# Streaming encoder layer on one core: the last two groups of h made beside the first four attention tiles, and the projections of the first unit given out on another plan

## The chip, the core and the metric

The kernel runs on one core of a Trainium2 chip. The metric is the device time of one execution in microseconds; the time of a kernel is the median over its runs. A separate execution is recorded by the hardware profiler, and all views below are of that one.

The engines are named as in the profile: PE is TensorE (matmuls; PEld its weight loads), DVE is VectorE, ACT is ScalarE, POOL is GpSimd, SP is SyncE, which here issues nearly all transfers, one after the other, on its own queue (SPq).

## The reference

One layer of a streaming encoder. 2048 new frames of one prompt, and 16 further frames of each of 8 running streams with 512 cached frames, go through the same weights.

```python
h, gate = adaln_modulate(x, c, norm_g, w_ada, b_ada)   # rms norm, then scale and shift per sequence
qa, ka, va, za, qb, kb, vb, zb, ga, gb = split(h @ w_in)
qa, ka = rope(qa, pos), rope(ka, pos)
oa = diff_attention(qa, ka, va, lam)            # 4 heads: softmax minus lambda times a second softmax
ob = stick_breaking_attention(qb, kb, vb)       # 8 heads: sigmoids and a running product of 1 - sigmoid
oa = rms_norm(oa, subln_g) * (1 - lam_init)
ya = (oa * silu(za)) @ w_branch_a
yb = (ob * silu(zb)) @ w_branch_b
x = x + gate * ((sigmoid(ga) * ya + sigmoid(gb) * yb) @ w_out)
y = rms_norm(x, final_g)
```

The outputs are y and the new keys and values of both branches. All tensors are 32-bit floats. The kernel keeps that precision on 16-bit matmuls: each operand is split into a high and a low half, and a product is the sum of three matmuls.

## The kernel before

**Tiles and units.** The prompt is 16 tiles of 128 rows; the 128 rows of the running streams are a seventeenth (index 16, `NT`). The heads are done in 8 units (`units`), in turn one diff-attention head and a pair of stick-breaking heads. A *step* is one tile of one unit; the list `steps` takes in each unit the sample tile first and then tiles 0 to 15, so step 0 is the sample tile of unit 0, step m (1 to 16) is tile m - 1 of unit 0, and step 17 begins unit 1: 136 steps.

**Projection.** `project` makes a step in 12 *pieces* of two matmuls of 512 columns (L423), 24 in all, into one of two PSUM banks ("mm"). In odd units 12 more pieces of two matmuls make a block of gate columns (L495). When the 24 are done, `finish` turns the bank into outputs and 16-bit operands: ScalarE copies (L437) and splits (L287, L450), VectorE makes the low halves (L292, L451), GpSimd does the rotation (L457 to L462), and three stores go out on SyncE's queue. `transpose_qk` (L508 to L519) turns q and k during the next step; its results for q live in six buffers (`Q_BUFS`).

**Where h comes from.** h, transposed and split, is made in the first stage in groups of four tiles. `normed(g)` sums squares and scales the rows of x (L1049). `modulated(g)` has eight pieces, one for each 128 columns: four transposes on TensorE (L1070), two ScalarE operations (L1076, L1077), one of VectorE (L1078). They fill one of two 16 KB buffers (`hp`); after the eighth piece SyncE writes the group to DRAM (`hT_d`, L1087). The projections of the first stage read h straight from `hp`, by the table `at_hand`; all others read it back into one of three buffers (`hs`) by `fetch_h` (L400). While `at_hand` is empty, each step issues the reading of the next one at its third piece (`H_AT`). Groups 0 and 2 share one `hp` buffer, 1 and 3 the other, so group 3 can be written only when the projections of tiles 4 to 7 have read theirs.

**Attention.** `attention(n)` returns two lists: the scores of step n (`scores`, L630 to L634; VectorE takes them out of PSUM, L545; softmax and weights on ScalarE and VectorE, L120, L594, L287, L292), and the products with V (`pv`, L678 to L683) of step n - 2 (`PV_LAG`). Between them the weights are transposed by a transfer on SyncE's queue (L568). In the first stage the scores of a tile lie in two of the four free weight buffers (`early_sc`), even tiles in one pair, odd ones in the other; later in a pool of its own.

**The order.** All pieces of projection stand in one list, `line`. `position(x)` is the place in it where step x begins, with a fraction for a part of a step. `take(target, need)` gives out pieces up to a target, or further if a tile's attention would otherwise lack its operands. `interleave` merges several lists in proportion to given costs. That fixes the order of the program. The framework's scheduler then orders each engine's instructions by a simulated timeline, with the program's order as priority, so that an instruction that is ready can go ahead of earlier ones that are not.

**The first stage** (`P0_AT`, `P0_STEPS`) makes groups 0 and 1 of h beside the projections up to position 5. Then, for each of attention tiles 0 to 7, it interleaves: a quarter of `modulated(2)` (two pieces) for tiles 0 to 3, a quarter of `modulated(3)` for tiles 4 to 7; `normed(3)` beside the first four; the last two parts of the modulation from `w_ada` (`gates`) beside tiles 4 and 6; and the pieces of projection up to the next target of `P0_STEPS`. At its end three tiles are read back by `fetch_h`.

**After it**, the loop over n from 9 gives each attention step its projections up to a target that follows a planned time: `past` adds a duration for each step so far, `pace` is that share of all 136 steps, and the target is `LEAD` (5) steps further. `prepare_unit(1)`, which loads unit 1's weights, sums their squares and cuts them in halves (L319, L321, L274, L289, L292), is given out over n = 9 to 12. The first four weight buffers it loads into are those that held the scores of the first stage.

Of the kernel before, what the change touches and what calls it, by code (L numbers as in the profile page):

```python
# [32 lines left out]
NT = SEQ // P  # L33
# [10 lines left out]
W_FIRST = 12  # L44
WIDE_BUFS = 6
P0_AT = 1.0, 5.0
P0_STEPS = 6.0, 7.0, 8.0, 9.0, 10.0, 11.0, 11.5, 12.0
K_BUFS = 6
V_BUFS = 23
S_TILES = 13  # L50
# [4 lines left out]
LEAD = 5.0  # L55
# [55 lines left out]
def layer_kernel(ctx: ExitStack, tc: tile.TileContext, a: dict):  # L111
# [751 lines left out]
    def position(x):  # L863

        m = min(int(x), len(steps) - 1)
        return starts[m] + (starts[m + 1] - starts[m]) * (x - m)

    def take(target, need):

        i = at[0]  # L870
        out = []
        while i < len(line) and (i < target or any(m <= need for m, _ in line[i : i + 14])):
            out.append((1.0, line[i][1]))
            i += 1
        at[0] = i
        return out
# [17 lines left out]
    with tc.tile_pool(name="p0", bufs=1) as p0:  # L894
# [136 lines left out]
        def normed(g):  # L1031

            t0, w = GROUPS[g]
            nt = w // P

            def square(i):
                if i == 0:
                    ss[g] = p0.tile([P, 4], F32, tag="ss", name="ss", bufs=2)
                sum_squares(xs[g][i], D, ss[g][:, i : i + 1])
                if i == nt - 1:  # L1040
                    ss[g] = rsqrt(ss[g], nt, D, p0, "rstd")

            def scale(i):
                x = xs[g][i]
                r = ss[g][:, i : i + 1]
                if g == 0 and i % 2:
                    V.tensor_scalar(out=x, in0=x, scalar1=r, scalar2=None, op0=ALU.mult)
                else:
                    G.tensor_scalar(out=x, in0=x, scalar1=r, scalar2=0.0, op0=ALU.mult, op1=ALU.add)  # L1049

            if g not in xs:
                xs[g] = load_x(t0 // P, nt)
            squared = [] if g in ss else [(0.5, lambda i=i: square(i)) for i in range(nt)]
            return squared + [(1.0, lambda i=i: scale(i)) for i in range(nt)]
# [36 lines left out]
        def gates():  # L1091

            def last():
                gateT = p0.tile([P, KT, 9], F32, name="gateT")
                V.tensor_tensor(out=gateT, in0=mod[:, 16:24, :],
                                in1=wide(bgT[:, 16:24]), op=ALU.add)
                gr = wide_tile().rearrange("p k n -> p (k n)")
                for n in range(2):
                    pt = bank("s")
                    for j in range(4):  # L1100
                        T.transpose(pt[0:9, j * P : (j + 1) * P], gateT[:, n * 4 + j, :], ident)
                    V.tensor_copy(out=gr[0:9, n * 512 : (n + 1) * 512], in_=pt[0:9, :])
                load(out=gate_d, in_=gr[0:9, 0:D])

            def piece(n):
                modulation(n)
                if n == 5:
                    last()

            return [(1.0, lambda n=n: piece(n)) for n in (4, 5)]  # L1110
# [7 lines left out]
        del free[:]  # L1118
        attention(0)
        for t, to in enumerate(P0_STEPS):  # L1120
            if t % 4 == 0:
                work, beside = modulated(2 + t // 4), normed(3) if t == 0 else gates()
            i = t % 4
            m = len(beside) // 4
            some = beside[i * m : i * m + m] if m else beside[i // 2 : i // 2 + 1] if i % 2 == 0 else []
            interleave(work[2 * i : 2 * i + 2], some, take(position(to), t + 2), *attention(t + 1))

        at_hand.clear()
        for m in range(3):
            fetch_h(*steps[int(P0_STEPS[-1]) + m])  # L1130

    free += early_sc
    del early_sc[:]
# [5 lines left out]
    whole = sum(duration(t) for _, t in steps)  # L1139
    first_step = len(P0_STEPS) + 1  # L1140
    past = sum(duration(t) for _, t in steps[:first_step])
    back += prepare_unit(1)
    cuts = None
    branch_weights = list(range(8))
# [125 lines left out]
    for n in range(first_step, len(steps) + PV_LAG):  # L1270
        if n < len(steps):
            u, t = steps[n]
            past += duration(t)
            if t == NT and u < 7:
                back += prepare_unit(u + 1)
            if u == 7 and not back and not spare and len(branch_weights) > 1:
                branch_weight()
            if back:
                for fn in back[: -(-len(back) // max(1, (W_READY if u else W_FIRST) - t % NT))]:
                    back.pop(0)()  # L1280
            else:
                for _ in spare[: -(-len(spare) // ((NT + 1 - t % NT) + 8 * (6 - min(u, 6))))]:
                    spare.pop(0)()
        qk, vs = attention(n)
        target = position(len(steps) * past / whole + LEAD)
        pieces = take(target, min(n + 1, len(steps) - 1))
        if at[0] == len(line) and not pieces and not spare:
            if cuts is None:
                cuts = early_work()
            pieces = [(1.0, fn) for fn in cuts[: -(-len(cuts) // (len(steps) + PV_LAG - n))]]  # L1290
            del cuts[: len(pieces)]
        interleave(pieces, qk, vs)
# [123 lines left out]
```

## Time and profile before

| | |
|---|---|
| median of 3 runs | 2296.72 us (2291.05 to 2299.35) |
| the profiled execution | 2301.96 us, span 2300.1 us |
| mean granted TensorE clock | 0.962 |
| busy: PE, DVE, ACT, POOL | 91%, 70%, 64%, 30% |
| last piece of h, group 3, written out from | 174.25 us |
| first projection with unit 1's weights | 223.60 us |
| first scores of unit 1 | 307.86 us |

A view by stretches gives the busy time of each engine between two times, counted from the first instruction; PEclk is the TensorE clock that was granted, 1.00 being full. In a timeline a line is a start, a duration, the engine, the source line, the operation, output and inputs, and in brackets the idle time of the engine just before with what ended it. A matmul's duration reaches into the next one's, so matmuls are compared by their spacing. In a list of waits the columns are the total, the number of times and the longest.

### The profile page before, as it was taken

How to read it: one execution, taken by the hardware profiler on the slowest of the kernel's cores; microseconds unless marked ns; L12 is line 12 of the kernel's file. 1: busy time of each engine (PE TensorE's matmuls, PEld its weight loads, DVE VectorE, ACT ScalarE, POOL GpSimd, SP SyncE). 2: the span in 40 equal slices, each digit the busy share in tenths (PEclk: the TensorE clock that was granted, in tenths of full speed). 3: DMA queues.
4: the chain of work that ended last, by engine and by line, in shares of the span. 5: the costliest groups of instructions: out<-in, count | busy, mean ns of one | idle time of the engine just before them, and what ended most of it. 6: DMA issues, size and time to landing. Idle time of an engine off the chain costs nothing. (4 is left out here: it accounts for less than half of the span.)

```text
span 2300.1 us, 40624 instructions
## 1 busy us (share of the span) xinstructions
PE 2088.9 (91%) x14478; PEld 1111.0 (48%) x14478; DVE 1609.4 (70%) x3523; ACT 1482.1 (64%) x2968; POOL 688.5 (30%) x575
## 2 busy tenths in 40 slices
PE   4997998998999899899989989999986789888997
PEld 2554554554555455455545555555553344444443
DVE  4576866689786677978666798877778655555554
ACT  3876767678776677777667787766776444444431
POOL 1522012345300234530023464113344222232331
PEclk7998999999999999999999999999997899999998
DMA  8659658597775768875566887657687979887662
GB/s 293 209 139 259 169 126 223 143 203 180 195 158 125 164 143 194 183 192 134 116 163 145 198 182 174 150 137 162 149 185 174 300 216 260 209 218 199 185 154 74
DMA packets 764555, 412.98 MB, mean 180 GB/s; under 512 B 525530, under 2 KB 709130, under 8 KB 763840
## 3 DMA queue, kind: packets, MB, share of 16 engines
q1 hardware_dynamic: 763274, 409.91, 72.7%
q8 instruction: 113, 1.85, 0.3%
q14 instruction: 90, 0.74, 0.1%
q10 hardware_dynamic: 1078, 0.48, 0.1%
HBM read 212.58 MB, written 72.91 MB: 124 GB/s over the span
## 5 line engine op out<-in xcount | busy, mean ns | idle before, releaser
L613 POOL TENSOR_TENSOR sc_p<-sc_p,sc_n 128x127 f32<-128x127 f32 (+7 forms) x192 | 307.4, 1605 | 791.6 <-DVE sc_n L607 775.7
L423 PE MATMUL ps_mm<-wb,hs 128*128 128x512 f16 x1632 | 415.8, 386 | 4.2 <-ACT gt L498 4.2
L423 PEld LDWEIGHTS <-hs 128*128 128x128 f16 x2976 | 263.7, 99 | 253.7 <-issue 23.2
L423 PE MATMUL ps_mm<-wa,hs 128*128 128x512 f16 x1344 | 335.8, 381 | 6.0 <-DVE v L292 4.7
L607 DVE TENSOR_TENSOR_SCAN sc_n<-ps_s,sc_n,zero_t 128x512 f32<-128x512 f32 x192 | 245.4, 1278 | 70.5 <-ACT ps_s L120 68.4
L120 ACT ACTIVATE sc_p<-ps_s,usc 128x512 f32<-128x512 f32 (+3 forms) x320 | 202.5, 633 | 104.8 <-PE ps_s L631 62.2
L630 PE MATMUL ps_s<-k,qst 128*128 128x512 f16 (+3 forms) x640 | 226.1, 354 | 45.7 <-DVE sc_n L607 33.5
L562 DVE TENSOR_TENSOR sc_n<-sc_p,sc_n 128x128 f16<-128x128 f32 (+7 forms) x192 | 213.6, 1118 | 43.0 <-ACT sc_n L561 42.6
L1335 PE MATMUL ps_o<-wo,wb 128*128 128x512 f16 x816 | 199.6, 400 | 30.3 <-DMA wb<-wa 25.5
L631 PE MATMUL ps_s<-k,qst 128*128 128x512 f16 (+3 forms) x640 | 226.3, 354 | 0.0
L682 PE MATMUL ps_o<-v,wt 128*128 128x128 f16 x1088 | 192.5, 225 | 26.2 <-DMA wt<-sc_n 26.0
L495 PE MATMUL ps_mm<-wa,hs 128*128 128x512 f16 x816 | 203.3, 379 | 1.2 <-DVE wa L292 1.2
L495 PE MATMUL ps_mm<-wb,hs 128*128 128x512 f16 x816 | 203.2, 379 | 0.0
L495 PEld LDWEIGHTS <-hs 128*128 128x128 f16 x1632 | 140.5, 98 | 123.4 <-issue 1.4
L120 ACT ACTIVATE ps_s<-ps_s,usc 128x512 f32<-128x512 f32 (+3 forms) x320 | 194.0, 606 | 0.0
L561 ACT CAST sc_n<-sc_p 128x128 f16<-128x128 f32 (+7 forms) x192 | 153.6, 804 | 57.3 <-POOL sc_p L613 57.1
L683 PE MATMUL ps_o<-v,wt 128*128 128x64 f16 x1088 | 174.0, 198 | 0.0
L682 PEld LDWEIGHTS <-wt 128*128 128x128 f16 x1088 | 107.3, 101 | 107.0 <-DMA wt<-sc_n 34.9
L1335 PEld LDWEIGHTS <-wb 128*128 128x128 f16 x816 | 81.9, 102 | 135.4 <-DMA wb<-wa 31.1
L457 POOL TENSOR_TENSOR rot<-pr,rope 128x256 f32<-128x256 f32 x68 | 64.2, 944 | 273.6 <-ACT pr L437 225.5
L683 PEld LDWEIGHTS <-wt 128*128 128x128 f16 x1088 | 105.3, 101 | 72.3 <-issue 1.9
L607 DVE TENSOR_TENSOR_SCAN sc_n<-ps_s,zero_t 128x128 f32<-128x128 f32 (+3 forms) x128 | 104.5, 818 | 48.1 <-ACT ps_s L120 46.4
(324 smaller groups left out, 4177.7 us busy)
## 6 DMA issues: line engine op xcount, KB each, us to landing
hs<-hT_d SPq DMA_DIRECT2D x124, 512.0 KB, 4.2
g_d<-gt SPq DMA_DIRECT2D x68, 256.0 KB, 4.1
out_dram<-pr SPq DMA_DIRECT2D x204, 64.0 KB, 1.9
wide<-in_w_ada_dram SPq DMA_DIRECT2D x12, 1024.0 KB, 9.9
wa<-in_w_in_dram SPq DMA_DIRECT2D x36, 256.0 KB, 5.5
z_d<-pr SPq DMA_DIRECT2D x136, 64.0 KB, 2.0
o_d<-o SPq DMA_DIRECT2D x136, 64.0 KB, 2.4
hs<-z_d SPq DMA_DIRECT2D x17, 512.0 KB, 4.1
```

Source lines behind the costliest of these rows:

```text
L120: i = S.activation(**kw)
L423: T.matmul(box["p"], box["h"][:, hi, k, :], U["w"][k][:, wi, :], start=(n == 0), stop=(n == 3 * KT - 1))
L495: T.matmul(box["g"][:, 0:gw], box["h"][:, hi, k, :], U["wg"][k // per][:, k % per, wi, :], start=(j == 0), stop=(j == 3 * KT - 1))
L561: S.copy(out=hi, in_=src)
L562: V.tensor_tensor(out=lo, in0=src, in1=hi, op=ALU.subtract)
L607: V.tensor_tensor_scan(out=dst[:, lo : lo + n][:, ::-1], data0=src[:, 0:n][:, ::-1], data1=zero_t[:, 0:1].to_broadcast([P, n]), initial=fi ...
L613: G.tensor_tensor(out=p[:, 0:m], in0=p[:, 0:m], in1=n[:, 1 : m + 1], op=ALU.mult)
L630: T.matmul(p[:, 0:n], qst[:, c, :], kk[:, c, 0:n], start=True, stop=False)
L631: T.matmul(p[:, 0:n], qst[:, 2 + c, :], kk[:, c, 0:n], start=False, stop=not diag)
L682: T.matmul(po[:, c * P : (c + 1) * P], wt[:, wj, :], vt[:, c, :, :], start=first, stop=False)
L683: T.matmul(po[:, c * P : c * P + 64], wt[:, nb + wj, :], vt[:, c, 0, :], start=False, stop=last)
L1335: T.matmul(po, st["y"][:, yi * 8 + k, :], wo[j * 4 + k // 2][:, wi, k % 2, :], start=(n == 0), stop=(n == 3 * KT - 1))
```

## The change

Four things, three in the first stage and one behind it:

- `modulated(2)` is made beside attention tiles 0 and 1, four pieces each, `modulated(3)` beside tiles 2 and 3; the two parts of `normed(3)` stand beside tiles 0 and 1, the two of `gates` beside tiles 4 and 5.
- The targets of projection go up to 14 instead of 12.
- After tile 4's part, the `at_hand` entries of tiles 13, 14 and 15 are dropped and these tiles are read back (`fetch_h`) at once; tile 12 is still taken from `hp`. The readings at the end of the stage are gone.
- For n below 17 the target goes from the last of `P0_STEPS` to 17 + `LEAD` in proportion to `pace`; from n = 17 on it is as before.

```diff
-P0_STEPS = 6.0, 7.0, 8.0, 9.0, 10.0, 11.0, 11.5, 12.0
+P0_STEPS = 7.0, 9.0, 10.0, 11.0, 12.0, 12.5, 13.0, 14.0
...
         for t, to in enumerate(P0_STEPS):
-            if t % 4 == 0:
-                work, beside = modulated(2 + t // 4), normed(3) if t == 0 else gates()
-            i = t % 4
-            m = len(beside) // 4
-            some = beside[i * m : i * m + m] if m else beside[i // 2 : i // 2 + 1] if i % 2 == 0 else []
-            interleave(work[2 * i : 2 * i + 2], some, take(position(to), t + 2), *attention(t + 1))
+            work, beside = [], []
+            if t in (0, 2):
+                both_halves, scaled = modulated(2 + t // 2), normed(3) if t == 0 else []
+            if t < 4:
+                work, beside = both_halves[t % 2 * 4 : t % 2 * 4 + 4], scaled[t % 2 * 4 : t % 2 * 4 + 4]
+            elif t < 6:
+                beside = gates()[t - 4 : t - 3]
+            interleave(work, beside, take(position(to), t + 2), *attention(t + 1))
+            if t == 4:
+                for m in range(3):
+                    at_hand.pop(NT - 3 + m)
+                    fetch_h(*steps[NT - 2 + m])

         at_hand.clear()
-        for m in range(3):
-            fetch_h(*steps[int(P0_STEPS[-1]) + m])
...
     past = sum(duration(t) for _, t in steps[:first_step])
+    start = len(steps) * past / whole
...
-        target = position(len(steps) * past / whole + LEAD)
+        pace = len(steps) * past / whole
+        if n < NT + 1:
+            target = position(P0_STEPS[-1] + (NT + 1 + LEAD - P0_STEPS[-1]) * (pace - start) / (NT + 1 - start))
+        else:
+            target = position(pace + LEAD)
```

## The prediction

> **What bounds the kernel now.** I read the page first, then the chain of waits, then busy time by stretch for the first 360 us, then TensorE's waits there, then the timelines of the engines around its longest gap.
>
> ```profile
> span 2300.1 us, 40624 instructions
> PE 2088.9 (91%) x14478; PEld 1111.0 (48%) x14478; DVE 1609.4 (70%) x3523; ACT 1482.1 (64%) x2968; POOL 688.5 (30%) x575
> ```
> ```profile
> 1839.00 1.28 DVE x L1348
> ```
>
> TensorE is busy 91%: its 211 us of idle time are all that an edit of the order can win. The chain of waits goes back from the end only to 1839 us (its first listed piece is above) and says nothing of the first stage, so that has to be read by stretches (columns: stretch, length, busy us of PE, PEld, DVE, ACT, POOL with counts, granted TensorE clock, share of the DMA engines, GB/s):
>
> ```profile
> core 0: us, PE busy (x) PEld busy (x) DVE busy (x) ACT busy (x) POOL busy (x), PEclk, DMA share, GB/s
> ...
> 100.00:131.00 31.00, 31.00 (x213) 17.12 (x210) 19.77 (x63) 25.37 (x59) 8.82 (x12) 1.00 0.54 176
> 131.00:156.00 25.00, 23.97 (x195) 13.55 (x194) 16.98 (x53) 19.20 (x43) 4.92 (x6) 1.00 0.74 201
> 156.00:164.00 8.00, 7.19 (x42) 3.89 (x43) 5.96 (x13) 3.71 (x10) 4.68 (x5) 1.00 0.41 89
> 164.00:190.00 26.00, 15.27 (x109) 9.52 (x108) 17.78 (x47) 15.35 (x30) 0.90 (x2) 0.74 0.65 184
> 190.00:242.00 52.00, 46.95 (x283) 23.85 (x281) 39.76 (x107) 37.32 (x79) 15.48 (x17) 0.97 0.90 252
> 242.00:300.00 58.00, 58.00 (x411) 32.10 (x410) 44.59 (x121) 39.25 (x78) 0.00 (x0) 1.00 0.70 154
> 300.00:360.00 60.00, 51.48 (x359) 28.52 (x358) 36.75 (x80) 42.76 (x93) 12.26 (x14) 0.93 0.61 142
> ```
>
> TensorE is full up to 131 us and from 242 to 300. Between, it idles 1.0 + 0.8 + 10.7 + 5.1 = 17.6 us, and it runs slowed: (1 - 0.74) x 15.27 + (1 - 0.97) x 46.95 = 5.4 us. **Together 23.0 us is the prize** of this part. TensorE's longest waits there (total, times, longest):
>
> ```profile
> PE ps_s L630 <- DVE sc_p L545: 5.0, 1, 5.0
> PE ps_o L678 <- DMA wt<-wa: 2.7, 2, 2.0
> PE ps_t L508 <- DVE fsq L333: 1.9, 1, 1.9
> ...
> PE ps_mm L423 <- DMA hs<-hT_d: 1.3, 1, 1.3
> PE ps_mm L495 <- DVE wa L292: 1.2, 1, 1.2
> ```
>
> These name whoever came last. Why there was nothing else to run is in the queue of SyncE, in the DMA issues of the stage (KB, us to landing) and in TensorE's timeline:
>
> ```profile
> 174.25 0.32 SPq L1087 DMA_DIRECT2D hT_d<-hp  x1
> ...
> 183.83 1.02 SPq L400 DMA_DIRECT2D hs<-hT_d  x2
> 184.90 7.80 SPq L319 DMA_DIRECT2D wa<-in_w_in_dram  x8
> ```
> ```profile
> hT_d<-hp SPq DMA_DIRECT2D x3, 2048.0 KB, 7.8
> ```
> ```profile
> 186.62 0.63 PE L630 MATMUL ps_s<-k,qst 128*128 128x512 f16 x1
> 187.04 0.63 PE L631 MATMUL ps_s<-k,qst 128*128 128x512 f16 x1
> ...
> 188.78 0.38 PE L630 MATMUL ps_s<-k,qst 128*128 128x512 f16 x1
> 188.99 0.38 PE L631 MATMUL ps_s<-k,qst 128*128 128x512 f16 x1
> ...
> 190.09 1.03 PE L423 MATMUL ps_mm<-wa,hs 128*128 128x512 f16 x4
> ...
> 204.93 7.04 PE L423 MATMUL ps_mm<-wa,hs 128*128 128x512 f16 x24 [1.32 <-DMA hs<-hT_d]
> ...
> 223.60 1.67 PE L423 MATMUL ps_mm<-wb,hs 128*128 128x512 f16 x7
> ```
> ```profile
> 156.62 5.34 PE L423 MATMUL ps_mm<-wa,hs 128*128 128x512 f16 x24
> ```
>
> The last group of h is written out at 174.25 and lands some 7.8 us later; its first tiles are read back at 183.83, and the first projection from them runs at 190.09. From 162 (the 24 matmuls at 156.62 are step 12, tile 11) to 190 no projection is at hand, only attention tiles, whose pace VectorE and the transposing transfers set. After the gap a 512-column matmul is 0.42 us apart from the next (186.62 to 187.04), later 0.21. The row at 156.62 also shows that the order is not the program's: by the planner's targets step 12 belongs beside tile 9. The scheduler takes what is ready, so moving pieces earlier matters only where nothing was ready.
>
> **The change, part by part.** I worked out the pieces (two matmuls each, 0.43 us by the spacing above) that the targets give. Beside attention tiles 0 to 7: before 12 12 12 12 12 12 6 6, after 24 24 12 12 12 6 6 12. Beside steps 9 to 16: before 0 9 16 17 18 37 41 43, after 9 10 11 17 25 26 29 29. The sums agree at step 16 (265 and 264), so from there on the program is as before. Nothing is computed anew; two readings of h (tiles 11 and 12) fall away, two issues of about 0.5 us (1.02 for two) on SyncE's queue. The gain can only be stall, so I ask how much of the 23.0 us stays.
>
> (a) *The front.* 24 more pieces (10.4 us) and the eight pieces of group 3's h come before the fifth attention tile. Rows of 90 to 180 us, per instruction:
>
> ```profile
> L1076 ACT ACTIVATE hp<-ps_s,ab 128x512 f16<-128x512 f32 x19 | 14.7, 773 | 8.9 <-PE ps_s L1070 8.8
> ...
> L1077 ACT ACTIVATE tmp<-hp,nb 128x512 f32<-128x512 f16 x19 | 13.7, 720 | 0.1
> ...
> L1070 PE MATMUL ps_s<-ident,wide 128*128 128x128 f32 x76 | 11.8, 275 | 0.3 <-DVE wa L545 0.3
> ...
> L437 ACT ACTIVATE pr<-ps_mm,usc 128x512 f32<-128x512 f32 x9 | 6.1, 680 | 1.5 <-PE ps_mm L423 1.5
> ...
> L519 ACT COPY qst<-ps_t 128x512 f16<-128x512 f16 x10 | 5.8, 576 | 0.0
> L450 ACT ACTIVATE qbuf<-rot,sq 128x256 f16<-128x256 f32 x11 | 5.6, 507 | 3.6 <-POOL rot L462 3.6
> ...
> L287 ACT ACTIVATE k<-rot,sq 128x128 f16<-128x128 f32 x11 | 4.3, 392 | 0.9 <-POOL rot L462 0.9
> ```
>
> ScalarE gets 8 x (0.77 + 0.72) = 11.9 us for h and 2 x 2.5 = 5.0 us for the two steps (four rows and a split of v like that of k): 17 us. TensorE gets at most 10.4 + 32 x 0.275 = 19 us, less where the transposes overlap: 11.8/76 is longer than their spacing, and I take half, so 15. ScalarE is already busy 25.4 of 31 us there. At that utilization (0.82) it needs 17/0.82 = 21 us and TensorE waits 6; with its gaps filled 2. I take **4**, bounds 0 and 8.
>
> (b) *Weights of unit 1.* They are loaded into the score buffers of the first stage, free only after tiles 6 and 7 have been transposed out of them: 184.90. VectorE cuts them
>
> ```profile
> 209.50 6.02 DVE L292 SCALAR_TENSOR_TENSOR wb<-wa,sw,wb 128x512 f16<-128x512 f32 x7
> ...
> 216.12 0.74 DVE L292 SCALAR_TENSOR_TENSOR wb<-wa,sw,wb 128x512 f16<-128x512 f32 x1
> ```
>
> so step 17 could run without a stop from about 212, 27 us after the first load; it did at 223.60, after step 16. All earlier work of TensorE is the same in both kernels; without the 23.0 us, less 1.2 us that lie behind 223.60 (the wait of L495), it would be done at 223.6 - 21.8 = 202, with (a) at 206. The change does not touch what starts these loads, and I see no reason to move 184.90 either way: group 3's h leaves VectorE and ScalarE before tiles 6 and 7, which frees their buffers sooner, but two more steps stand before those tiles. So TensorE meets the end of its work at 206 and the weights at 212: **6** kept; bounds 0 (loads 6 us sooner) and 14 (8 us later). This stall stands where none was seen before.
>
> (c) *Waits of the weights' chain itself*: fsq 1.9 and L495 on wa 1.2 have their cause in the loads and stay: **3**, bounds 1 and 4.
>
> (d) *Three readings beside the fifth tile.* Their issues replace others. On SyncE's queue they stand behind the write of group 3; what is queued behind them are the transposes of tiles 4 to 7 and the stores, and P·V of those tiles waits for the transposes. If SyncE stands until the write has landed it is 7.8 us once; if the write was issued long before, 0. In this trace the same pair cost
>
> ```profile
> SPq L400 <- DMA hT_d<-hp: 1.0, 1, 1.0
> ```
>
> and I take **1**, being nearest to that row. The buffer wait of VectorE's first writes to the new score buffers (the 5.0 us) has its cover: group 3's write would be over, and step 13's last matmuls stand earlier on TensorE.
>
> (e) *Pacing of the first unit.* It gives 36 pieces more by step 13 and takes them back by step 16. From 242 to 300 TensorE was 58.00 of 58.00 busy although the targets were lower then, so the scheduler had covered for it: **0**; bounds -3 and +4, what the idle 8.5 us of the stretch from 300 could give or take.
>
> Kept: 4 + 6 + 3 + 1 = 14. **Gain 23 - 14 = 9 us.** The profiled execution took 2301.96 us (span 2300.1), so 2293; the median of the runs is 2296.72, 5.2 below it, so I forecast **2288**.
>
> On the clock, the row first: after the 5.0 us wait TensorE was at half pace and still so at 186.62; at 204.93 24 matmuls took 7.04 instead of 5.34. The Trainium skill (TensorE: Matmul & The Clock Gate, "Part 1: The HAM clock gate") says that an idle window of about 3.4 us halves the clock until a similar time of work. The trace agrees for the long gap; the 1.32 us wait before 204.93 is too short for that rule alone. The rule speaks against the change in one place: were (b) one gap of 6 us, it would add about 2 us (estimated from that page), a gain of 7 instead of 9.
>
> **The rivals.** *Nearly all the prize is won* (chance 0.20): tile 6's buffers are free earlier, the loads move ahead, (b) is 0 and (a) 2: a gain of 17 to 18, 2279. For it: ScalarE and VectorE still made group 3's h between 164 and 174. Against: eight loads at a DMA share of 0.90 in the next stretch.
>
> *Nothing is won* (0.22): (b) is 14 or more, or group 3's h cannot be made sooner since its buffer is held by tiles 4 to 7 until step 8's last matmul. TensorE idles at 206 to 222 instead of at 172 to 190: 2296. For it: unit 1's weights were used within 12 us of being ready.
>
> *Slower* (0.13), one mechanism: the last attention tiles of the stage come later. Two more steps (10.4 us) and (a)'s 4 us stand ahead of tile 7, its transposes leave 14 us later and the loads start at 199 instead of 185; step 17 runs at 226 and its gates follow. That is 3 us later than before, and with SyncE held for 7.8 us before those transposes 11: 2300 to 2308. It decides from loads later than about 196. Against: TensorE was idle 10.7 us right there, so the two steps find room.
>
> **How the numbers follow.** The forecast has 0.45 and its own range 2281 to 2295. A measurement of this kernel can tell about 0.5% (11.5 us) from no change: faster means below 2285.2, slower above 2308.2. Faster: 0.30 of the forecast, all of the first rival: 0.135 + 0.20 = 0.33. Slower: half of the last rival and a little for what lies outside: 0.09. Same: 0.58. The range takes the first rival with (c) and (e) at their good ends (gain 23) and the slower one to its middle: 2273 to 2303.
>
> **What would show it.** Write of group 3 issued near 150 instead of 174.25 and the three readings before 165; no wait of several us of TensorE between 164 and 190, clock near 1.0; ScalarE over 0.85 busy from 100 to 140 (a); the first load of unit 1's weights within 179 to 191, and a wait just before the first L423 matmul on wb (b); that matmul at about 214 instead of 223.60. Wrong if that matmul is later than 223.6, or if it is early and the first scores of unit 1 are not.

## The result, and the profile after

The changed kernel takes 2291.6 us (median of 20 runs, 2287.9 to 2299.3), the kernel before 2295.6 (20 runs, 2291.1 to 2299.4) beside it on the same chip. The ratio is **0.9979**, 95% interval 0.9971 to 0.9987: a gain of 0.21%, some 4.8 us, below the 0.5% that the prediction set as the bound of "no change". The forecast was a gain of 9.

The profiled execution of the changed kernel took 2288.94 us. It lies 3 us below the median of its kernel and that of the kernel before 6 us above, so the two spans differ by 13 us where the medians differ by 4. I therefore read from the pair *where* the time goes, and take sizes from the medians.

The page of the changed kernel, span and busy time:

```profile
span 2287.2 us, 40620 instructions
PE 2083.3 (91%) x14478; PEld 1111.4 (49%) x14478; DVE 1606.7 (70%) x3523; ACT 1483.5 (65%) x2968; POOL 689.8 (30%) x575
```

The same stretches as in the prediction (length, busy us of PE, PEld, DVE, ACT, POOL, granted clock, DMA share, GB/s), changed kernel:

```profile
100.00:131.00 31.00, 31.00 (x203) 18.16 (x202) 17.83 (x53) 26.71 (x58) 9.62 (x14) 1.00 0.57 182
131.00:156.00 25.00, 23.54 (x190) 12.59 (x188) 16.30 (x47) 18.36 (x43) 5.70 (x9) 1.00 0.61 202
156.00:164.00 8.00, 8.00 (x58) 4.79 (x57) 6.01 (x13) 3.37 (x9) 2.60 (x3) 1.00 0.97 286
164.00:190.00 26.00, 25.50 (x174) 13.71 (x172) 20.08 (x55) 15.90 (x33) 8.17 (x9) 1.00 0.75 201
190.00:242.00 52.00, 40.14 (x265) 23.18 (x264) 46.42 (x139) 41.79 (x89) 7.24 (x8) 0.84 0.72 172
242.00:300.00 58.00, 54.81 (x350) 29.68 (x349) 37.29 (x91) 32.46 (x65) 0.00 (x0) 0.97 0.65 146
300.00:360.00 60.00, 54.86 (x387) 30.08 (x386) 38.30 (x84) 48.12 (x104) 13.73 (x15) 0.97 0.77 198
```

The hole at 164 to 190 is gone: 25.50 of 26 us busy at full clock, where before 15.27 at 0.74 stood. A new one stands right behind it: from 190 to 242 TensorE now idles 52 - 40.14 = 11.9 us and loses 0.16 x 40.14 = 6.4 to the clock, 18.3 us together, where before it lost 6.5. Its waits between 96 and 242 us (total, times, longest):

```profile
PE ps_o L678 <- DMA wt<-wa: 4.6, 1, 4.6
PE ps_t L210 <- DVE col L281: 3.2, 1, 3.2
PE ps_o L678 <- ACT wb L287: 1.5, 1, 1.5
...
PE ps_mm L423 <- DVE wb L292: 0.4, 1, 0.4
```

As before, a wait names who came last, not what was missing. What was missing shows in the queue of SyncE and in the timelines of ScalarE, VectorE and TensorE (L319 loads the q, k and v weights, L321 the gate weights; `sg` is the scale of the gate weights), changed kernel:

```profile
148.22 0.38 SPq L1087 DMA_DIRECT2D hT_d<-hp  x1
...
156.07 1.27 SPq L400 DMA_DIRECT2D hs<-hT_d  x3
...
165.02 0.90 SPq L321 DMA_DIRECT2D wb<-in_w_in_dram  x2
...
185.06 2.09 SPq L319 DMA_DIRECT2D wa<-in_w_in_dram  x4
188.82 0.44 SPq L319 DMA_DIRECT2D wa<-in_w_in_dram  x1
190.25 1.29 SPq L319 DMA_DIRECT2D wa<-in_w_in_dram  x2
192.00 4.58 SPq L568 DMA_TRANSPOSE wt<-wa  x1
196.63 1.12 SPq L319 DMA_DIRECT2D wa<-in_w_in_dram  x2
```
```profile
205.77 1.05 ACT L274 ACTIVATE junk<-wa 128x1024 f16<-128x1024 f32 x1
...
222.36 1.04 ACT L274 ACTIVATE junk<-wb 128x1024 f16<-128x1024 f32 x1
```
```profile
232.12 0.16 DVE L225 TENSOR_SCALAR sg<-sc_e 128x2 int32<-128x2 int32 x1
```
```profile
216.78 0.63 PE L423 MATMUL ps_mm<-wb,hs 128*128 128x512 f16 x1
...
233.71 0.38 PE L495 MATMUL ps_mm<-wa,hs 128*128 128x512 f16 x1
233.92 5.34 PE L423 MATMUL ps_mm<-wb,hs 128*128 128x512 f16 x24
...
307.37 0.22 PE L630 MATMUL ps_s<-k,qst 128*128 128x128 f16 x1
```

and the same places of the kernel before:

```profile
193.69 2.14 SPq L321 DMA_DIRECT2D wb<-in_w_in_dram  x4
```
```profile
212.84 1.05 ACT L274 ACTIVATE junk<-wb 128x1024 f16<-128x1024 f32 x1
```
```profile
229.12 1.67 PE L495 MATMUL ps_mm<-wa,hs 128*128 128x512 f16 x7
```

Group 3 of h is written out 26 us earlier and the three tiles are read back at 156. Unit 1's weights start at 185.06 as before (184.90), but by count only seven of the eight loads go by 191.5; the eighth is behind a transpose that holds the queue for 4.58 us (before, all eight went in 7.80 us). ScalarE's last sum over the q, k and v weights runs at 205.77, that over the gate weights at 222.36 (before 212.84). The first projection with the new weights comes at 216.78 instead of 223.60, 7 us early. **But the gain is lost again between 190 and 260 us**, at two operands. From 190 to 216.78 no projection runs, for want of q, k and v weights. Then the gate block: unit 1 is the first unit with gate columns, its gate block (L495) needs weights that are cut last, and it starts at 233.71, 4.6 us *later* than before (229.12). The projections of the next step stand behind it on TensorE. The loads are not what makes the gate block late: the gate weights are loaded from 165.02, before from 193.69. It is their sums, in ScalarE's order, and the scale worked out from them, which VectorE finishes at 232.12 (before at 223.92), 9 us after the last sum. At the first scores of unit 1 the two kernels are level, 307.37 against 307.86.

How far ahead TensorE is can be counted. A projection matmul (L423, L495) costs 0.216 us (24 of them took 5.34 at 233.92, the last one's 0.38 reaching into the next), a P·V matmul 0.056 by its spacing, a pair of scores about 0.4 (an estimate: two matmuls, 0.21 apart at 512 columns, less for the narrow ones). Counts of L423 up to 190 us, kernel before and kernel after (L495 has none yet):

```profile
0.00:190.00 190.00, 76.37 (x312) 0.88 0.69 218
```
```profile
0.00:190.00 190.00, 97.38 (x408) 0.94 0.73 235
```

408 is 17 steps of 24: all projections of unit 0 are done by 190. TensorE's work done, in us at full clock, worked out from such counts (a_oldpace and a_oldwg are experiments below):

| up to | before | after | a_oldpace | a_oldwg |
|---|---|---|---|---|
| 190 us | 86.9 | 105.2 | 103.2 | 104.8 |
| 224 us | 114.5 | 119.3 | 117.4 | 134.4 |
| 242 us | 130.1 | 135.0 | 130.1 | 148.7 |
| 260 us | 147.6 | 148.3 | 147.3 | 166.3 |
| 300 us | 186.4 | 187.0 | 186.4 | 205.5 |
| 360 us | 234.6 | 239.2 | 235.0 | 254.0 |
| 480 us | 349.3 | 357.7 | 350.4 | 373.5 |

The first stage wins 18 us by 190. Of that 13.5 are given back by 224, before the gate block has begun in either kernel, and the rest between 242 and 260. The changed kernel gets its lasting lead only after 300, where a_oldpace, which lacks the new targets, gets hardly any.

### The profile page after: what moved, and what is told of

It is laid out like the page before. It is cut to its first block, busy times and chain, and to the rows that moved or that the text cites. A ratio compares the mean times of both kernels' runs of the same rounds, so it can differ in the third digit from the quotient of the medians.

```text
span 2287.2 us, 40620 instructions
## 1 busy us (share of the span) xinstructions
PE 2083.3 (91%) x14478; PEld 1111.4 (49%) x14478; DVE 1606.7 (70%) x3523; ACT 1483.5 (65%) x2968; POOL 689.8 (30%) x575
## 4 chain that ended last, share of the span: by engine, by line
PE 57%; DVE 13%; DMA 9%; ACT 8%; issue 8%; POOL 3%; SPq 1%; POOLq 0%; DVEq 0%; ACTq 0%
PE ps_mm L423 20%; PE ps_mm L495 12%; PE ps_mm L1207 5%; PE ps_o L1344 5%; PE ps_s L630 3%; PE ps_s L631 3%; DVE sc_n L607 3%; DMA wt<-sc_n 2%; ACT junk L274 2%; ACT sc_p L120 1%; PE ps_o L682 1%; DMA wb<-wa 1%; POOL sc_p L613 1%; DMA hs<-o_d 1%; DVE wb L292 1%
## 5 line engine op out<-in xcount | busy, mean ns | idle before, releaser
L423 PE MATMUL ps_mm<-wb,hs 128*128 128x512 f16 x2244 | 559.6, 382 | 7.3 <-DVE v L292 3.9
L423 PEld LDWEIGHTS <-hs 128*128 128x128 f16 x2928 | 256.7, 98 | 237.1 <-issue 14.8
L495 PE MATMUL ps_mm<-wa,hs 128*128 128x512 f16 x1224 | 307.4, 379 | 0.0
L607 DVE TENSOR_TENSOR_SCAN sc_n<-ps_s,sc_n,zero_t 128x512 f32<-128x512 f32 x192 | 245.5, 1279 | 68.2 <-ACT ps_s L120 66.1
L495 PEld LDWEIGHTS <-hs 128*128 128x128 f16 x1632 | 140.2, 98 | 119.7 <-issue 0.5
L683 PE MATMUL ps_o<-v,wt 128*128 128x64 f16 x1088 | 173.3, 197 | 0.0
L423 PE MATMUL ps_mm<-wa,hs 128*128 128x512 f16 x684 | 168.9, 379 | 0.0
L607 DVE TENSOR_TENSOR_SCAN sc_n<-ps_s,zero_t 128x128 f32<-128x128 f32 (+3 forms) x128 | 104.6, 818 | 47.4 <-ACT ps_s L120 46.1
L274 ACT ACTIVATE junk<-wa 128x1024 f16<-128x1024 f32 (+1 forms) x73 | 66.7, 914 | 103.9 <-POOL wa L1211 66.5
```

The lines of the kernel that those rows point to most:

```text
L423: T.matmul(box["p"], box["h"][:, hi, k, :], U["w"][k][:, wi, :], start=(n == 0), stop=(n == 3 * KT - 1))
L495: T.matmul(box["g"][:, 0:gw], box["h"][:, hi, k, :], U["wg"][k // per][:, k % per, wi, :], start=(j == 0), stop=(j == 3 * KT - 1))
L607: V.tensor_tensor_scan(out=dst[:, lo : lo + n][:, ::-1], data0=src[:, 0:n][:, ::-1], data1=zero_t[:, 0:1].to_broadcast([P, n]), initial=fi ...
L683: T.matmul(po[:, c * P : c * P + 64], wt[:, nb + wj, :], vt[:, c, 0, :], start=False, stop=last)
```

## The experiments

Theories. **W**: the first stage's gain is eaten by the waits on unit 1's weights; were they ready, it would stay. **V**: the attention of unit 0, at the pace of VectorE and the transposes, sets the time up to 300 us whatever the projections do. **P**: what gain there is comes from the new targets behind the stage, which the prediction's (e) had at 0. All ratios are to the kernel before, run beside it on the same chip, with their 95% intervals.

### The parts alone

`a_oldpace`: the changed kernel with the old targets behind the stage.

```diff
-        if n < NT + 1:
-            target = position(P0_STEPS[-1] + (NT + 1 + LEAD - P0_STEPS[-1]) * (pace - start) / (NT + 1 - start))
-        else:
-            target = position(pace + LEAD)
+        target = position(pace + LEAD)
```

> The changed kernel without the new targets for n below 17 (the pacing of before). By the prediction's step (e), the pacing is worth nothing: 2291.6 +- 2. Rival P (the gain comes from the pacing, since the two profiles are level in projections at 300 us and differ only after that): about 2295.6.

Measured: 2296.03 us, **1.0002** (0.9989 to 1.0014). The three first-stage parts together are worth nothing that can be told, though by 190 us they put TensorE 16 us ahead (table).

`b_newpace`: the kernel before with the new targets only (the same lines added to it, with `start`).

> The kernel before with only the new targets for n below 17, starting from its own 12. Step (e): 2295.6 +- 2. Rival P: about 2291.6.

Measured: 2293.73 us, 0.9991 (0.9977 to 1.0004): between the two, not to be told from none by itself. The new targets give the whole gain of the changed kernel, but perhaps only half of it without the new first stage; the intervals don't decide that.

`a_pacelin`: the changed kernel, targets with the same end but in equal steps.

```diff
-            target = position(P0_STEPS[-1] + (NT + 1 + LEAD - P0_STEPS[-1]) * (pace - start) / (NT + 1 - start))
+            target = position(P0_STEPS[-1] + (NT + 1 + LEAD - P0_STEPS[-1]) * (n + 1 - first_step) / (NT + 1 - first_step))
```

> The changed kernel with the first unit's targets rising by the same number of steps beside each tile instead of by planned time; the end point is the same. It tests whether the 4 us that the new pacing is worth are its mechanism (pieces handed out ahead, so that unit 1's softmax, scales and weights of unit 2 are ready earlier) or the chance of another order in the scheduler. Mechanism: the pieces are still handed out ahead of the old targets, and the ratio stays at 0.997 to 0.999 of the kernel before. Chance: anywhere between 0.995 and 1.001, with the order of TensorE's instructions from 320 to 420 us unlike that of the changed kernel.

Measured: 2292.73 us, **0.9988** (0.9979 to 0.9997). It lies between the new targets (0.9979) and the old ones (1.0002) on the same first stage, and its interval overlaps both. That agrees with P, but it does not rule out the chance of a lucky order, whose forecast, anywhere from 0.995 to 1.001, holds this value too. For P the evidence is `a_oldpace`: its interval (from 0.9989) lies just clear of that of the changed kernel (to 0.9987).

### Unit 1's weights earlier

`a_wbfirst`: the first four buffers that unit 1's weights are loaded into are not the score buffers of the stage but new ones, which nothing has to leave. `b_wbfirst` does the same to the kernel before.

```diff
-    free += early_sc
-    del early_sc[:]
...
     free += buffers_of_4k("wb", 8)
+    free += early_sc
+    del early_sc[:]
```

> The changed kernel, but unit 1's weights are loaded first into the eight new weight buffers, not into those that hold the scores of tiles 6 and 7. Theory W (in the changed kernel TensorE runs out of projections at 190 us and waits for unit 1's weights, whose loads wait for those score buffers): the first load of the weights goes out near 165 instead of 185.06 us, the first L423 matmul on wb comes near 200 instead of 216.8, TensorE's idle and slowed time from 190 to 242 falls from 18 us to under 10, and the time falls by 7 to 13 from 2291.6: 2279 to 2285. Theory V (VectorE, busy 46.4 of 52 us from 190 to 242, is what paces that stretch): the loads go out early all the same, but the time stays within 2 us of the changed kernel: 2289.5 to 2293.5.

> The same edit on the kernel before. Theory W: there the projections of unit 0 last until 223.6 us, so the weights are not what TensorE waits for; 0 to -3 us against 2295.6. Theory V: no change either, 0 +- 2. A gain of 5 or more would say that the edit is worth something by itself, whatever the change did.

Measured: 2288.2 us, **0.9965** (0.9951 to 0.9978), and on the kernel before 2295.93, 0.9998 (0.9986 to 1.0011). If the buffers are worth something (3 us against the changed kernel by the ratios, whose intervals overlap), it is only where the projections are ahead. TensorE and SyncE in `a_wbfirst`:

```profile
165.93 1.34 SPq L319 DMA_DIRECT2D wb<-in_w_in_dram  x2
```
```profile
205.88 0.61 PE L423 MATMUL ps_mm<-wb,hs 128*128 128x512 f16 x1
...
211.89 4.48 PE L423 MATMUL ps_mm<-wb,hs 128*128 128x512 f16 x20 [2.60 <-DVE wb L292]
...
235.06 0.38 PE L495 MATMUL ps_mm<-wb,hs 128*128 128x512 f16 x1
```

Loads 19 us earlier, the first projection 11 us earlier, and then the 24 projection matmuls of step 17 are done by 216.4 and no projection follows until the gate block at 235.06. The loads came as W forecast and the first projection 6 us after its 200, but what TensorE idles or runs slowed from 190 to 242 stayed at 18.6 us (37.07 us busy at a clock of 0.90), where W had under 10, and the time fell between the two forecasts: the first wait is removed, and the second one, on the gate weights, takes its place.

`a_wbfirst_w9` gives out the preparation of unit 1's weights wholly beside step 9 (`W_FIRST = 9`, was 12).

> The changed kernel with unit 1's weights loaded first into the eight buffers that nothing has to leave (loads from 166 us, as in the run a_wbfirst), and with W_FIRST 9 instead of 12, so that ScalarE's sums over the weights and VectorE's cuts are given out wholly beside step 9 instead of step 12. Theory W (the time is lost where the projections of unit 1 wait for their weights): the first matmul on the new weights comes at 195 to 202 instead of 205.88, TensorE is over 40 of 52 us busy from 190 to 242 at a clock above 0.95, and the time falls below the 0.9965 of a_wbfirst, to 0.993 to 0.9955. Theory V (what the first stage wins is given back later, because the attention tiles of unit 0 go at the pace of VectorE and the transposes): the first matmul comes earlier too, but the first scores of unit 1 stay at 304 to 308 us and the ratio at 0.9955 to 0.998.

Measured: 2289.24 us, 0.9968 (0.9958 to 0.9978), no different from `a_wbfirst`; its first projection with the new weights came at 207.71, not earlier, and its gate block at 231.30. The condition of theory W's forecast was not met, so this decides nothing between W and V. But it shows what the gate block waits for. ScalarE's last sum over the gate weights and the scale made from the sums:

```profile
210.27 1.04 ACT L274 ACTIVATE junk<-wa 128x1024 f16<-128x1024 f32 x1
```
```profile
228.54 0.16 DVE L225 TENSOR_SCALAR sg<-sc_e 128x2 int32<-128x2 int32 x1
```

The sums end 12 us earlier than in the changed kernel, and the gate block comes only 2.4 us earlier. In between stands a chain of small VectorE operations (about 0.15 us each) and one small matmul, strewn from 216.11 to 228.54 among VectorE's work for the softmax.

### The waits taken away

`a_oldw` projects the first four steps of unit 1 (17 to 20) with unit 0's weights and scales, whose buffers are given back later for it.

```diff
+        W = units[0] if U["u"] == 1 and t in (NT, 0, 1, 2) else U
+        if W is not U:
+            sc, sq = W["sc"], W["sq"]
...
-            T.matmul(box["p"], box["h"][:, hi, k, :], U["w"][k][:, wi, :], start=(n == 0), stop=(n == 3 * KT - 1))
+            T.matmul(box["p"], box["h"][:, hi, k, :], W["w"][k][:, wi, :], start=(n == 0), stop=(n == 3 * KT - 1))
...
-            if u > 0:
+            if u > 1:
                 free.extend(units[u - 1]["bufs"])
...
+            if t == NT and u == 1:
+                free.extend(units[0]["bufs"])
             if t == NT and u < 7:
```

> The changed kernel, but steps 17 to 20 (unit 1, the first four h tiles) are projected with unit 0's weights and scales, whose buffers are freed four steps later; so unit 1's part of the output is computed with other weights for those tiles, and nothing waits for unit 1's weights at 190 us; the same number of matmuls runs. Theory W: no stretch without projections from 190 to 216, what TensorE is idle or slowed from 190 to 242 falls from 18 us to under 8, and the time to 0.991 to 0.995 of the kernel before. Theory V: the stretch is filled, but the first scores of unit 1 stay at 304 to 308 us, TensorE idles 6 us or more in a later stretch before 420 us, and the ratio is 0.996 to 0.999.

Measured: 2291.96 us, 0.9981 (0.9973 to 0.9990), as the changed kernel. The ratio by itself looks like V. But the stretch was not filled, as both theories had it: from 190 to 242 TensorE was busy 33.84 us at a clock of 0.77. Its timeline shows why:

```profile
201.47 0.81 PE L426 MATMUL ps_mm<-wa,hs 128*128 128x512 f16 x3
...
235.14 0.58 PE L498 MATMUL ps_mm<-wa,hs 128*128 128x512 f16 x1 [4.16 <-POOL wa L289]
235.52 1.06 PE L426 MATMUL ps_mm<-wa,hs 128*128 128x512 f16 x2
```

Step 17 is projected before 203 and then the gate block (L498 here) stands until 235.14, behind the cut of the gate weights by GpSimd. The wait was moved, not removed: the gate weights alone are enough to eat the first stage's gain. (Whether the q, k and v weights alone would be was not tried.) So the next run takes the gate weights out too.

`a_oldwg`: as `a_oldw`, and the gate blocks of steps 17 to 20 use unit 0's q, k and v weights and scale.

```diff
-                T.matmul(box["g"][:, 0:gw], box["h"][:, hi, k, :], U["wg"][k // per][:, k % per, wi, :], start=(j == 0), stop=(j == 3 * KT - 1))
+                wg = W["w"][k][:, wi, :] if W is not U else U["wg"][k // per][:, k % per, wi, :]
+                T.matmul(box["g"][:, 0:gw], box["h"][:, hi, k, :], wg, start=(j == 0), stop=(j == 3 * KT - 1))
...
-                S.activation(out=gt[:, 0:gw], in_=box["g"][:, 0:gw], func=AF.Identity, scale=U["sc"][:, 6:7])
+                S.activation(out=gt[:, 0:gw], in_=box["g"][:, 0:gw], func=AF.Identity, scale=sc[:, 1:2] if W is not U else sc[:, 6:7])
```

> As the run a_oldw, but here the gate blocks of steps 17 to 20 too take unit 0's weights and scale (unit 0 has no gate weights, so its q, k and v weights stand in, the same number of matmuls of the same shape). In a_oldw the wait had only moved: the gate block of step 17 stood at 235.14 us behind the cut of the gate weights, and the projections of step 18 behind it. Now nothing of unit 1's weights is needed before step 21; unit 1's part of the output is wrong for those tiles, gates too. Theory W (the waits on unit 1's weights and gate weights eat what the first stage wins): no stretch of 10 us without projections from 190 to 242, TensorE's work done by 242 us 10 us or more above the changed kernel's, and the ratio 0.990 to 0.995. Theory V (the attention chain of unit 0 sets the end of this stretch, projections only fill): the work done is ahead at 242 and no longer ahead by 400, and the ratio is 0.9965 to 0.999.

Measured: 2273.58 us, **0.9899** (0.9883 to 0.9915): theory W, just past the good end of what it forecast. The stretches:

```profile
164.00:190.00 26.00, 26.00 (x181) 14.12 (x179) 19.56 (x55) 16.03 (x35) 7.42 (x9) 1.00 0.77 203
190.00:242.00 52.00, 47.08 (x303) 24.60 (x302) 43.16 (x130) 44.03 (x94) 7.56 (x9) 1.00 0.68 183
242.00:300.00 58.00, 57.47 (x450) 33.62 (x449) 46.50 (x119) 43.76 (x86) 1.77 (x2) 1.00 0.78 165
```
```profile
201.03 1.46 PE L499 MATMUL ps_mm<-wa,hs 128*128 128x512 f16 x6 [1.00 <-DVE v L292]
```

The gate block (L499 here) starts at 201.03, the clock is 1.00 throughout, and of 18.3 us lost between 190 and 242 there remain 4.9. TensorE's lead over the kernel before is 17.9 us at 190 and 18.7 at 260, 24.2 at 480 (table): **what the first stage wins is kept when unit 1's weights are not waited for.** V, which had this lead gone by 400, is refuted. The attention chain can go faster: VectorE is 89.7 us busy from 190 to 300 (in the changed kernel 83.7), and the first scores of unit 1 come at 287.44 instead of 307.37.

`a_dve10` puts 12 us more on VectorE in the attention of unit 0, the changed kernel otherwise.

```diff
+                if job["U"]["u"] == 0 and 8 <= job["t"] < NT and seg is segs[0]:
+                    for i in range(2):
+                        V.scalar_tensor_tensor(out=extra, in0=p[:, 0:512], scalar=r[:, 0:1], in1=p[:, 512:1024], op0=ALU.mult, op1=ALU.subtract)
```

> The changed kernel with two more VectorE operations of 512 columns (0.74 us each by the cuts of the weights) in the softmax of attention tiles 8 to 15 of unit 0, into a tile that nobody reads: 16 operations, 12 us. Theory V (attention of unit 0, at VectorE's pace, sets the time up to 300 us): 7 to 12 us slower than the changed kernel, 1.001 to 1.0035 of the kernel before, and the first scores of unit 1 5 us or more later. Theory W: VectorE has room (46 of 52 us busy from 190 to 242, 37 of 58 after): 0 to 3 us slower, 0.998 to 0.9995, the first scores of unit 1 within 3 us.

Measured: 2295.43 us, 0.9992 (0.9982 to 1.0002). Against 0.9979 that is 3 us slower, though the two intervals overlap a little. The ratio is in W's range; the first scores of unit 1 are 7 us late (314.71 against 307.37), as V said. By the medians VectorE costs about a quarter of the 12 us that are put on it here: not the bound, and not free either.

### Towards a better kernel

`a_gfirst`: `a_wbfirst`, and in unit 1 the gate weights are loaded and summed right behind the q, k and v weights, ahead of the cuts.

```diff
+        if u == 1:
+            pieces = pieces[0:4] + [lambda k=k: norm("g", k, k // gk) for k in range(0, KT, gk)] + [bounds, bounds_g] + pieces[5:]
+            pieces += [lambda k=k: gate_cut(k) for k in range(0, KT, gk)]
-        if gw:
+        elif gw:
```

> The run a_wbfirst (unit 1's weights first into the eight free buffers), and in unit 1 the loads and sums of the gate weights are given out right behind those of the q, k and v weights, ahead of the cuts, so that all eight loads go into free buffers at 166 us. In a_wbfirst the projections of unit 1 ran from 205.88 to 216 and then stood until 235.06 behind the gate weights. Theory W: the first gate matmul comes at 212 to 222 instead of 235, and the ratio falls from 0.9965 to 0.992 to 0.9955. Theory V: the gate matmuls come as early, and the ratio stays at 0.996 to 0.998.

Measured: 2287.01 us, **0.9948** (0.9932 to 0.9964), the size that W forecast, but not by the mechanism that it named. ScalarE and TensorE:

```profile
202.92 1.04 ACT L274 ACTIVATE junk<-wb 128x1024 f16<-128x1024 f32 x1
...
215.35 1.04 ACT L274 ACTIVATE junk<-wb 128x1024 f16<-128x1024 f32 x1
...
220.77 1.04 ACT L274 ACTIVATE junk<-wb 128x1024 f16<-128x1024 f32 x1
```

The gate weights are loaded at 175, but ScalarE sums three of the four only at 215 to 222, among the softmax of unit 0, and the gate block starts at 234.8 as in `a_wbfirst`. Its work done by 480 us is within 1 us of that of `a_wbfirst`. What it gains on `a_wbfirst` (0.9965) has no place that I could find in the first 480 us, and the two intervals overlap.

`a_gfirst_w9` is `a_gfirst` with `W_FIRST = 9`.

> The run a_gfirst with W_FIRST 9 instead of 12: loads, sums, scales and cuts of unit 1's weights and gate weights are all given out beside step 9. In a_gfirst the gate weights lay in the chip from about 180 us, but ScalarE summed three of the four only at 215.35 to 221.9, and the first gate matmul came at 234.8, no earlier than in a_wbfirst (235.1). Theory W: with the sums given out earlier the gate matmuls start at 215 to 226, TensorE is over 44 of 52 us busy from 190 to 242, its work done by 242 us is 4 us or more above the 133.2 of a_gfirst, and the ratio falls below 0.9948, to 0.990 to 0.9940. If the attention chain sets the end after all: the gate matmuls come earlier and the ratio stays at 0.9945 to 0.9965.

Measured: 2285.81 us, 0.9945 (0.9930 to 0.9961), as `a_gfirst`. The gate block came at 232.3, 2.5 us earlier. The earlier place in the program moved two of ScalarE's sums over the gate weights to 205.73 and 211.51, but the last one only from 220.77 to 217.90, and the scale came at 228.45, 9.5 us after that sum. Both kernels beat the changed one by some 7 to 8 us and the one before by 12. Of the 18 us that `a_oldwg` shows to be there, more than half is left. By the timelines it should lie in ScalarE's eight sums and, by `a_wbfirst_w9`, in the small VectorE operations behind them; no run here moved those, so that is not shown.

### What the new targets do

`a_oldpace_ns`: `a_oldpace`, with the sums over branch and output weights given out from unit 2 on. With the old targets their loads go out just ahead of two transposes at 352 us, with the new ones 10 us earlier.

```diff
-            else:
+            elif u > 1:
                 for _ in spare[: -(-len(spare) // ((NT + 1 - t % NT) + 8 * (6 - min(u, 6))))]:
```

> The run a_oldpace (the changed kernel with the old targets of the first unit, ratio 1.0002), with the loads and sums of the branch and output weights given out from unit 2 on instead of from unit 0 on; nothing is left out. With the old targets four of these loads are issued at 346.7 to 351.6 us and two transposes behind them take 6.6 us (TensorE busy 5.3 of 10 us from 350 to 360); with the new ones the loads go at 336.8 to 345 us and each transpose takes 1.3. Theory C (the new pacing wins by getting these loads out of the way of the transposes): without them before 360 us TensorE is over 8 of 10 us busy from 350 to 360, and the ratio is 0.9975 to 0.999, as with the new pacing. Theory P (it wins because the projections of unit 1 are ahead of their attention tiles): the gap at 350 us stays within 2 us of what it was, and the ratio is 0.9995 to 1.001.

Measured: 2301.67 us, 1.0016 (1.0005 to 1.0027). The gap is as it was, as P said, and the time is a little above P's range. But theory C is not refuted by it, since its condition was not met: other loads, of unit 2's weights, came into the place of those that were taken away.

```profile
346.34 3.08 SPq L319 DMA_DIRECT2D wb<-in_w_in_dram  x5
...
351.05 1.94 SPq L319 DMA_DIRECT2D wb<-in_w_in_dram  x3
353.25 4.00 SPq L568 DMA_TRANSPOSE wt<-sc_n  x2
```

The two transposes behind them take 4.00 us instead of the 6.57 of `a_oldpace`, and TensorE is busy no more for it, which speaks against C but does not settle it. TensorE in `a_oldpace`, in `a_oldpace_ns`, and in the changed kernel (length, busy, clock, DMA share, GB/s):

```profile
350.00:360.00 10.00, 5.27 (x23) 0.76 1.07 285
```
```profile
350.00:360.00 10.00, 4.41 (x29) 0.81 1.04 243
```
```profile
350.00:360.00 10.00, 8.51 (x40) 0.83 1.11 293
```

In the kernel before and with the old targets TensorE stops here five times, for scores (`sc_n` L607, `qst` L519), transposes (`k` L292) and last for ScalarE's copy of a gate block (`gt` L498), and has no projection to put between. With the new targets the copy is not waited for, 14 more projection matmuls are done by 340 (765 against 751) at the same count of scores, and VectorE's cuts of unit 2's weights start at 334.50 instead of 344.22. That agrees with P. Which of these brings the others about, and how much of the gain is C's, was not tried and stays open.

## Why the prediction was right or wrong

The time lay in the range and in the forecast's own 2281 to 2295, a change within 0.5%, but that is in good part luck. Of the prize of 23.0 us the forecast left 14 as stall. Measured in the same way, 20.2 us of stall were left from 100 to 242, and another 4.8 came from 242 to 300, where there had been none, so nothing of the prize was won there. The gain came from a term that stood at 0. Two steps were wrong, (b) and (e), and their errors partly cancelled.

**The prize**, 23.0 us, was read rightly and is there: 18 us of lead at 190, and `a_oldwg`, which keeps it, ends 23 us (1.01%) under the kernel before. If the new targets are worth the same there as in the changed kernel, which no run separates, some 5 of that are theirs.

**(a) The front**, 4 us kept, was too much: from 100 to 164 TensorE idles 1.5 us (25.00 - 23.54). ScalarE took the additional work in its gaps and is busy for 0.86 of the time from 100 to 140, but TensorE had enough else to run. The stretch of the changed kernel:

```profile
100.00:140.00 40.00, 40.00 (x260) 23.46 (x258) 23.14 (x68) 34.26 (x76) 13.18 (x18) 1.00 0.61 200
```

**(b) Weights of unit 1**: the start of their loads (185.06 against an unmoved 184.90) and the first projection with them (216.78 against 214) came as worked out. What fell is the size, 6 us kept, bounds 0 and 14: the stretch from 190 loses 18.3. There are two reasons. I let the chain end with the q, k and v weights, "so step 17 could run without a stop from about 212"; the gate weights end it, whose sums and cuts come 17 us after, and half of step 17's 48 matmuls need them. The rows of before had a sign of it: the 1.2 us wait of L495, which I put into (c) as a term of its own. And I had the whole chain stand still while the work ahead of it moved. It came later: the eighth load of the q, k and v weights went behind a transpose, and the gate block 4.6 us later than before. The first did not cause the second: in `a_wbfirst`, with all eight loads out by 173.3, the gate block came at 235.06. The sentence "wrong if ... it is early and the first scores of unit 1 are not" names what happened.

**(c)** 1.9 for fsq became 3.2 for the sums of the same chain (`ps_t L210 <- col`); right in kind, and part of the same wait. **(d)**, taken at 1, cost nothing that shows: the three readings were issued in 1.27 us at 156.07, SyncE stood 2.3 us for the write of group 3 before them, and no wait of TensorE lies behind them.

**(e) Pacing**, taken at 0, is worth the whole gain of the changed kernel: 1.0002 without it against 0.9979 with it, some 5 us, more than the 3 that I had as its good end. I argued from 242 to 300, where TensorE was full; the new targets bear on the 8.5 us of idle time behind 300, which I quoted and used only as a bound.

**The rivals.** For the first stage alone, *nothing is won* came true, with its time (2296) and its mechanism: the hole moves from 164 to 190 to the stretch behind. I had it at 0.22 because I read "unit 1's weights were used within 12 us of being ready" as one piece of evidence among several; it was the deciding row. *Slower* has part of its mechanism (a transpose at 192.00 with the last load behind it at 196.63), not its price.

**On the clock**, the rows: with waits of 4.6 and 3.2 us the stretch from 190 ran at 0.84; in `a_oldwg`, whose longest wait there is 1.2 us, at 1.00. This agrees with the rule of the Trainium skill (TensorE: Matmul & The Clock Gate, "Part 1: The HAM clock gate") that an idle window of some 3.4 us halves the clock. The price was 6.4 us, three times the 2 that I worked out from that page for a single gap: there were several. The rows go beyond the rule, though: from 350 to 360 us the changed kernel was granted 0.83 with no wait above 1.4 us.

## What to carry to other kernels

A stall that is filled by doing work earlier moves to the next thing that the work runs into; before counting the gain, follow the *last* operand that the next block needs (here the gate weights, summed 17 us behind the first ones), not the first, and through every small operation up to its use. Where taking a wait away changes nothing, look whether it only moved to the next operand of the same block before concluding that the engine is bound elsewhere: one more operand turned 0.998 into 0.990. And a part of a change that moves no work in the stretch one looks at can still be what pays, in the stretch behind.

## What the runs showed of the hardware

A transposing transfer that stands close behind loads held SyncE's queue for longer here. Two at 352 us in the kernel before, behind five issues of loads, and the two at the same place of the changed kernel:

```profile
351.95 7.50 SPq L568 DMA_TRANSPOSE wt<-sc_n  x2
```
```profile
347.58 1.34 SPq L568 DMA_TRANSPOSE wt<-sc_n  x1
...
350.11 1.35 SPq L568 DMA_TRANSPOSE wt<-sc_n  x1
```

That is 3.75 us each, behind five loads issued within 5.2 us, against 1.35, behind two or three loads spread over 6 us. The number of loads alone does not set it: in `a_oldpace_ns` two transposes behind eight loads took 2.00 each. Whatever is queued behind pays for it, here stores and the readings of h; I had allowed for SyncE's queue in (d) and not in (b), where the 4.58 us at 192.00 put the last load of unit 1's weights back.
